# Norm factors of a differential attention spread over the partitions by TensorE transposes, with another planned order of the kernel's steps

## The chip, the cores and the metric

The kernel runs on one core of a Trainium2 chip. That core has five engines which run side by side, each through a list of instructions of its own in a fixed order: TensorE (PE, matrix products; PEld are its weight loads), VectorE (DVE), ScalarE (ACT), GpSimd (POOL), and SyncE (SP), which here issues the DMA transfers. An instruction that needs another engine's result waits for it, and everything behind it on the same engine waits too. The metric is the time of one execution on the device in microseconds (us); smaller is better.

## The reference, cut to what matters

One layer over 1024 positions of width 1024, in f32. One input projection feeds two groups of heads: group A (8 heads of 64) attends over its own chunk and 8 chunks to the left with a position bias, group B (4 heads of 128) subtracts two softmax maps, normalises each head's output by its root mean square, and both are gated, joined, projected and normalised.

```
s = q k^T * scale                  # two maps n = 0, 1 per head of group B
a = softmax(s0) - lam * softmax(s1)
o = a v                            # 128 values per head and position
o = o * rsqrt(mean(o^2) + eps) * subln_g * (1 - lam_init)
y_b = o * silu(g_b)
out = layer_norm(alpha * x + concat(y_a, y_b) @ w_out)
```

The rsqrt factor is one number per head and position.

## The kernel before, in words

Every f32 operand of a large product is split in a high part and a remainder (`xh` and `xl`, `wh` and `wl`, `pth` and `ptl`), and each product is made of two or three fast matmuls of such parts. ACT writes the high part (a cast), DVE or POOL subtracts it from the operand to give the remainder. A call on `nc.either` leaves it to the planner which of the two does it.

The program is first recorded and then ordered by a planner (`_Recorder`). Every operation gets a rank from its place in the recording (`SLOPE`), from the work that hangs on it and from its step's entry in `BIAS`; `_Recorder.schedule` then plays the program through with a cost for each operation and a delay, `HOP`, for a result that goes from one engine to another, and each engine takes the ready operation of the lowest rank. What comes out is the fixed order of each engine. `STEPS` names the steps in the order of recording: `qk_a0` to `qk_a3` project queries and keys of group A's four pairs of heads, `v_a`, `g_a` values and gates, `at_a` the attention, the same with `b` for group B, `wo` loads the output weights, `out0` makes group A's half of the output projection and `fin0` the other half with the last normalisation. Names of tiles carry their step's name: `at_b_ob` is tile `ob` of an `at_b` step, `qk_a_pj` the PSUM tile of a projection.

In an attention block the scores `sp` go to PSUM, DVE takes their maximum `nm`, ACT the exponent `p`; PE transposes `p` in 128x128 blocks into one PSUM bank `tp` (there is one buffer of it), ACT casts it to `pth`, DVE subtracts to `ptl`, and PE multiplies both with the values into `ya` (group A) or `ob` (group B). These two share one PSUM buffer (`yp`), so the next block's product starts only when the last reader of this one is through. While a block's chain runs over the other engines, PE does matmuls of other steps: projections, or `out_po` and `fin_po` of the output.

Group B's norm stands at the end of `attend_b`, once for each of four blocks of 256 positions and each of four heads, 16 times. ACT squares the output to `sq`, PE sums it over the partitions with a column of ones (so the sums stand with a position on each partition, `at_b_ob` 128x1), DVE scales them into `l0`, POOL raises them to the power -1/2. The output itself has its positions along the free dimension, so the factors must be spread as rows over all partitions: ACT multiplies the identity with each of two columns of `l0` (`dg`, two 128x128 diagonals), and PE multiplies a matrix of ones with both. DVE then applies the result to `yt`.

Of the kernel before, what the change touches and what calls it, by code (L numbers as in the profile page):

```python
# [12 lines left out]
F32 = mybir.dt.float32  # L13
# [5 lines left out]
P = 128  # L19
# [4 lines left out]
W = 512  # L24
# [4 lines left out]

HOP = dict(tensor=54, vector=36, scalar=36, gpsimd=80, sync=60)
ARRIVE = 1920.0
SLOPE = 165.1
CUTS = (0, 384, 512, 1024)
# [1 line left out]
LATE = 1600.0  # L37
SPARE = 420.0
BIAS = {
# [3 lines left out]
}  # L43

FIRST = "w0 x0 w2 w1 x1 w3 x2 x3 x4 x5 x6 x7".split()
WARM = 10
IN_TURN = {"m", "yp"}
BUFS = dict(small=5, y=4, stk=9, v=6, wr=4, wh=4, wl=4, p=4, ptl=2, pth=2, h=4, g=1, bt=1, tm=1, dg=1, s=2, yp=1, t=1, m=2)
STEPS = (
    "qk_a0 g_a0 init0 v_a0 g_a1 at_a0 qk_a1 at_a1 v_a1 qk_a2 g_a2 at_a2 qk_a3 g_a3 at_a3 qk_b0 g_b0 v_b0 "  # L50
    "at_b0 qk_b1 g_b1 at_b1 qk_b2 qk_b3 g_b2 v_b1 at_b2 g_b3 wo0 out0 wo1 at_b3 fin0"
).split()


# [89 lines left out]
def _cost(engine, fn, args, kw):  # L144

    out = args[0]
    n = out.width if isinstance(out, _View) else W
    psum = any(a.tile.psum for a in args if isinstance(a, _View))
    if engine == "tensor":
        if fn == "transpose":  # L150
            return 115, 190
        n = args[2].width
        if args[1].dtype == F32:
            return max(4 * n * 0.4167, 230), 205
        return max(11 + n * 0.4167, 112), 185
    if engine == "scalar":
        given = sum(isinstance(v, _View) for v in (*args[2:], kw.get("scale"), kw.get("bias"))) * 98
        n = max(n, args[1].width)
        return (65 if psum else 97) + 0.835 * n + given + (64 if "accum_out" in kw else 0), 100 + (50 if "accum_out" in kw else 0)
    if engine == "vector":  # L160
        if fn == "memset":
            return 25 + 0.1 * n, 85
        if fn in ("tensor_reduce", "bn_stats"):
            return 75 + 1.04 * args[1].width, 85
        if fn == "reciprocal":
            return 80 + 4 * n, 75
        if fn in ("tensor_scalar", "tensor_copy") and not psum:
            return 72 + 0.52 * n, 80
        return 72 + 1.04 * n, 85
    if engine == "gpsimd":  # L170
        if fn == "memset":
            return 40 + 0.9 * n, 50
        if fn == "tensor_scalar":
            return 250 + 0.84 * n + 83 * sum(isinstance(v, _View) for v in args[2:4]), 50
        if len(args) > 3 and args[3] == ALU.pow:
            return 500 + 85 * n, 40
        return 150 + 2.12 * n, 50
    return 50, 0
# [10 lines left out]
class _Recorder:  # L189
# [14 lines left out]
    def add(self, engine, fn, args, kw):  # L204
# [39 lines left out]
        for t in op.tiles:  # L244
            t.uses += 1
        (op.cost, op.lag), op.rank, op.start = _cost(engine, fn, args, kw), self.bias, None
        self.ops.append(op)

# [17 lines left out]
    def schedule(self):  # L266
# [19 lines left out]
        while len(order) < len(ops):  # L286
            again = False
            for e in self.ENGINES:
# [22 lines left out]
                if got.engine != e:  # L311
                    got.engine, (got.cost, got.lag) = e, _cost(e, got.fn, got.args, got.kw)
# [20 lines left out]
                for to in {x for s in got.succ for x in ops[s].either}:  # L333
                    heapq.heappush(events, (end if to == e else done + HOP[to], got.n, to))
                heapq.heappush(events, (done + (0 if e == "sync" else 60), got.n, "free"))
# [35 lines left out]
def hybrid_kernel(  # L371
# [18 lines left out]
    core, nc = tc.nc, _Recorder(tc)  # L390
# [3 lines left out]
    def pool(name, space="sbuf", bufs=None):  # L394
        n = bufs or BUFS[name]
        made = ctx.enter_context(tc.tile_pool(name="p_" + name, bufs=n, **spaces.get(space, {})))
        return _Pool(nc, made, n, space)
# [3 lines left out]
    y_pool, stk_pool, v_pool = pool("y"), pool("stk"), pool("v")  # L401
    wr_pool, wh_pool, wl_pool = pool("wr"), pool("wh"), pool("wl")
    p_pool, ptl_pool, pth_pool, h_pool, g_pool = pool("p"), pool("ptl"), pool("pth"), pool("h"), pool("g")
    bt_pool, tm_pool, dg_pool = pool("bt"), pool("tm"), pool("dg")
    sm_pool, st_pool = pool("small"), pool("stats", bufs=2)
    d_pool = pool("dram", "dram", 1)
    ps_s, ps_y, ps_m, ps_t = pool("s", "psum"), pool("yp", "psum"), pool("m", "psum"), pool("t", "psum")
# [1 line left out]
    ident = c_pool.tile([P, P], F32, "ident")  # L409
    make_identity(core, ident.get())  # L410
    ones = c_pool.tile([P, P], F32, "ones")
# [161 lines left out]
    def scores(stack, i, k0, w):  # L573

        q, k, kl = stack
        n = w if w <= W else W if w - W >= 256 else 384
        at = W - n if w > W else 0
        sp = ps_s.tile([P, 2 * W], F32, "sp", tag="s")
        block = slice(i * P, (i + 1) * P)
        for a, b in ((0, n), (n, w)):  # L580
            if a < b:
                keys, cols = slice(k0 + a, k0 + b), slice(at + a, at + b)
                nc.tensor.matmul(sp[:, cols], q[:, block], k[:, keys], start=True, stop=False)
                nc.tensor.matmul(sp[:, cols], q[:, block], kl[:, keys], start=False, stop=True)
        return sp[:, at : at + w]

    def exponent(sv, w, total):

        nm = sm_pool.tile([P, 1], F32, "nm", tag="nm")
        nc.vector.tensor_reduce(nm, sv, AX.X, ALU.max, negate=True)  # L590
        pt = p_pool.tile([P, S], F32, "p", tag="p")[:, :w]
        nc.scalar.activation(pt, sv, AF.Exp, bias=nm[:, 0:1], accum_out=total)
        return pt
# [66 lines left out]
    def attend_b(stacks, vt, yt):  # L660
        for g in range(4):
            ps = []
            l0, l1, cc = [sm_pool.tile([P, 2], F32, f"l{m}", tag=f"l{m}") for m in range(3)]
            for i in (2 * g, 2 * g + 1):
                w, u = (i + 1) * P, slice(i % 2, i % 2 + 1)
                es = []
                for m in range(2):
                    sv = scores(stacks[m], i, 0, w)
                    nc.vector.memset(sv[0:64, w - 64 : w], NEG)
                    es.append(exponent(sv, w, (l0, l1)[m][:, u]))  # L670

                p0, p1 = es
                nc.vector.reciprocal(l1[:, u], l1[:, u])
                nc.gpsimd.tensor_scalar(cc[:, u], l1[:, u], l0[:, u], nlam, ALU.mult, ALU.mult)
                nc.vector.scalar_tensor_tensor(p0, p1, cc[:, u], p0, ALU.mult, ALU.add)
                ps.append(p0)

            op = ps_y.tile([P, W], F32, "ob", tag="yp")
            o = op[:, :256]
            parts = []  # L680
            for k, us, hi, lo in transposed(ps, (0, 0), 2 * g + 2):
                parts += [(k, us, 0, hi), (k, us, 1, hi), (k, us, 0, lo)]
            for n, (k, us, part, pt) in enumerate(parts):
                nc.tensor.matmul(op[:, us], vt[k // 4][:, k % 4, part, :], pt, start=n == 0, stop=n == len(parts) - 1)

            cols = slice(g * 256, (g + 1) * 256)
            sq = tm_pool.tile([P, 256], F32, "sq", tag="tm")
            nc.scalar.square(sq, o)
            nc.vector.tensor_tensor(yt[:, cols], yt[:, cols], o, ALU.mult)
            nc.gpsimd.tensor_tensor(l0, l0, l0, ALU.mult)  # L690
            for u in range(2):
                nc.tensor.matmul(op[:, 256 + u : 257 + u], sq[:, u * P : (u + 1) * P], ones[:, 0:1], start=True, stop=True)

            nc.vector.scalar_tensor_tensor(l0, op[:, 256:258], 1.0 / (P * EPS), l0, ALU.mult, ALU.add)
            nc.gpsimd.tensor_tensor(l0, l0, mhalf, ALU.pow)
            dg = dg_pool.tile([P, 2, P], F32, "dg", tag="dg")
            for u in range(2):
                nc.scalar.mul(dg[:, u], ident, l0[:, u : u + 1])
            bc = op[:, 256:W]
            nc.tensor.matmul(bc.rearrange("p (u q) -> p u q", u=2), ones, dg, start=True, stop=True)  # L700
            nc.vector.scalar_tensor_tensor(yt[:, cols], yt[:, cols], gs[:, 0:1], bc, ALU.mult, ALU.mult)

    def gate(c0, yt):
# [73 lines left out]
    def at_b(p):  # L777
        attend_b(stacks["b", p], vb[p], yts["b", p])
# [173 lines left out]
```

## Time and profile before

| | us |
|---|---|
| median of 3 runs (679.42 to 681.44) | 679.81 |
| the profiled execution | 680.56 |
| its span, from the first to the last instruction | 678.8 |
| PE busy in it | 653.1 (96%) |
| PEld, DVE, ACT, POOL busy | 556.6, 410.0, 326.4, 328.9 |

The profiled execution's time is 1.8 us more than its span. A matmul's busy time includes a tail in which the next one already streams, so a busy PE may still have lost time between two starts. The granted clock of TensorE is 0.995 of full speed over the span; the slices of the page show it below 1.0 only at the very beginning and end.

### The profile page before, as it was taken

The page shows a single profiled execution, that of the slowest core. Times are in us where ns is not written, and L with a number is a line of the kernel's source. Part 1 is how long each engine was busy: PE and PEld are TensorE (multiplying, and loading weights), DVE is VectorE, ACT ScalarE, POOL GpSimd, SP SyncE. Part 2 cuts the span into 40 slices and gives each one's busy share as a digit, 9 for nine tenths or more (in the row PEclk, how much of TensorE's full clock was granted, in tenths as well). Part 3 has the DMA queues.
Part 4 walks back from the last instruction along what each step waited for, and adds up shares of the span by engine and source line. Part 5 has one row for each costly group of instructions (what it writes and reads, how often), then busy time and mean ns, then how long its engine had stood idle before and what let it go on. Part 6 is the DMA issues. An engine that isn't in the chain of part 4 may idle for free. (4 is left out here: it accounts for less than half of the span.)

```text
span 678.8 us, 10866 instructions
## 1 busy us (share of the span) xinstructions
PE 653.1 (96%) x3812; PEld 556.6 (82%) x3812; DVE 410.0 (60%) x839; ACT 326.4 (48%) x733; POOL 328.9 (48%) x367
## 2 busy tenths in 40 slices
PE   7899999999999999999999999999999999999993
PEld 7789878899888778787998788888798787878873
DVE  3521387777426764886248766842517957677875
ACT  5521466555335653665237546653416645454321
POOL 6620444434324443477225662677804736536673
PEclk8999999999999999999999999999999999999998
DMA  9433301400341125013320141125304643030121
GB/s 313 119 97 109 95 23 29 117 14 9 94 117 39 41 55 170 25 48 94 94 63 27 52 110 47 47 53 135 92 18 136 184 148 124 16 94 31 63 94 62
DMA packets 57855, 55.92 MB, mean 82 GB/s; under 512 B 5176, under 2 KB 44872, under 8 KB 57800
## 3 DMA queue, kind: packets, MB, share of 16 engines
q1 hardware_dynamic: 57800, 55.22, 27.1%
q8 instruction: 30, 0.49, 0.3%
q14 instruction: 25, 0.20, 0.1%
HBM read 36.32 MB, written 7.88 MB: 65 GB/s over the span
## 5 line engine op out<-in xcount | busy, mean ns | idle before, releaser
L367 POOL TENSOR_SCALAR at_a_p<-at_a_p,at_a_ls 128x640 f32<-128x640 f32 (+2 forms) x64 | 42.5, 666 | 49.2 <-DVE at_a_ls L367 42.0
L367 ACT ACTIVATE at_b_p<-at_b_sp,at_b_nm 128x128 f32<-128x128 f32 (+7 forms) x64 | 47.4, 743 | 26.3 <-DVE at_b_nm L367 20.4
L367 PE MATMUL fin_po<-wo_wo,fin_ys 128*128 128x512 f32 (+1 forms) x264 | 53.7, 356 | 4.0 <-DVE fin_z L367 2.7
L367 ACT ACTIVATE at_a_p<-at_a_sp,at_a_nm 128x640 f32<-128x640 f32 (+2 forms) x64 | 42.5, 664 | 24.8 <-DVE at_a_nm L367 15.2
L367 DVE TENSOR_TENSOR at_a_ptl<-at_a_tp,at_a_pth 128x512 fp32r<-128x512 f32 (+2 forms) x72 | 43.0, 597 | 16.1 <-ACT at_a_pth L367 15.2
L367 PEld LDWEIGHTS fin_po<-wo_wo,fin_ys 128*128 128x128 f32 x264 | 42.4, 189 | 10.9 <-DVE fin_z L367 3.2
L367 DVE TENSOR_REDUCE at_b_nm<-at_b_sp 128x1 f32<-128x128 f32 (+7 forms) x64 | 48.4, 757 | 2.1
L367 ACT CAST at_a_pth<-at_a_tp 128x512 fp32r<-128x512 f32 (+2 forms) x72 | 36.9, 512 | 22.1 <-PE at_a_tp L367 19.3
L367 PE MATMUL out_po<-wo_wo,out_ys 128*128 128x512 f32 x168 | 46.1, 404 | 0.0
L367 DVE TENSOR_REDUCE at_a_nm<-at_a_sp 128x1 f32<-128x640 f32 (+2 forms) x64 | 42.0, 656 | 1.7
L367 PE MATMUL at_a_ya<-at_a_pth,v_a_v 128*128 128x256 f32 x144 | 41.3, 287 | 1.4 <-DVE at_a_tm L367 0.9
L367 PE MATMUL at_a_tp<-k_ident,at_a_p 128*128 128x128 f32 x240 | 40.6, 279 | 1.0 <-DVE at_a_ptl L367 1.0
L367 POOL TENSOR_TENSOR g_a_ya<-g_a_ya,at_a_tm 64x256 f32<-64x256 f32 x32 | 23.9, 748 | 34.8 <-DVE at_a_tm L367 28.6
L367 PE MATMUL at_a_ya<-at_a_ptl,v_a_v 128*128 128x256 f32 x144 | 39.7, 305 | 0.4 <-DVE at_a_ptl L367 0.2
L367 PE MATMUL qk_b_pj<-k_xh,qk_b_wl 128*128 128x512 f32 x128 | 40.1, 403 | 0.0
L367 PE MATMUL qk_b_pj<-k_xl,qk_b_wh 128*128 128x512 f32 x128 | 39.0, 401 | 0.0
L367 PE MATMUL qk_b_pj<-k_xh,qk_b_wh 128*128 128x512 f32 x128 | 38.7, 401 | 0.0
L367 PE MATMUL v_b_pv<-v_b_wh,k_xh 128*128 128x256 f32 x128 | 36.3, 284 | 1.0 <-DVE g_b_yb L367 1.0
L367 PE MATMUL v_a_pv<-v_a_wh,k_xh 128*128 128x256 f32 x128 | 36.4, 284 | 0.0
L367 PE MATMUL v_a_pv<-v_a_wh,k_xl 128*128 128x256 f32 x128 | 36.3, 284 | 0.0
L367 PE MATMUL v_a_pv<-v_a_wl,k_xh 128*128 128x256 f32 x128 | 36.3, 283 | 0.0
L367 PE MATMUL v_b_pv<-v_b_wh,k_xl 128*128 128x256 f32 x128 | 36.2, 283 | 0.0
(170 smaller groups left out, 1912.0 us busy)
## 6 DMA issues: line engine op xcount, KB each, us to landing
xload_xr<-in_xt_dram SPq DMA_DIRECT2D x8, 512.0 KB, 7.4
qk_b_wr<-in_w_in_dram SPq DMA_DIRECT2D x16, 256.0 KB, 2.8
qk_b_r<-qk_b_r SPq DMA_DIRECT2D x64, 64.0 KB, 2.0
wo_wor<-in_w_out_dram SPq DMA_DIRECT2D x16, 256.0 KB, 2.7
out_z<-in_x_dram SPq DMA_DIRECT2D x14, 256.0 KB, 4.5
out_dram<-out_z SPq DMA_DIRECT2D x14, 256.0 KB, 2.0
qk_a_wr<-in_w_in_dram SPq DMA_DIRECT2D x12, 256.0 KB, 2.7
g_a_wr<-in_w_in_dram SPq DMA_DIRECT2D x8, 256.0 KB, 3.2
```

The costliest lines, as they stand in the source:

```text
L367: fn(*[real(a) for a in o.args], **{k: real(a) for k, a in o.kw.items()})
```

## The change

The spread of the factors loses ACT's two multiplications, the tile `dg` and the product with ones. Instead, PE transposes twice: its operand is a column of `l0` read with a step of zero along the free dimension, so each of 128 columns is the same one, and the transpose (against the identity, as for `p`) writes the factors as rows on all partitions, at the same place in PSUM. The rest of the chain is unchanged.

The planner's delay to TensorE rises from 54 to 304, so it plans every operand from another engine to reach PE 250 ns later; its cost of a transpose goes from 115 to 110. Four entries of `BIAS` change, and `STEPS` is reordered: `at_a0` is recorded ahead of `g_a1`, `v_a1` ahead of `at_a1`, `v_b1` ahead of `qk_b3` and `g_b2`.

```
-HOP = dict(tensor=54, vector=36, scalar=36, gpsimd=80, sync=60)
+HOP = dict(tensor=54 + 250, vector=36, scalar=36, gpsimd=80, sync=60)
...
-    "qk_a0 g_a0 init0 v_a0 g_a1 at_a0 qk_a1 at_a1 v_a1 qk_a2 g_a2 at_a2 qk_a3 g_a3 at_a3 qk_b0 g_b0 v_b0 "
+    "qk_a0 g_a0 init0 v_a0 at_a0 g_a1 qk_a1 v_a1 at_a1 qk_a2 g_a2 at_a2 qk_a3 g_a3 at_a3 qk_b0 g_b0 v_b0 "
...
         if fn == "transpose":
-            return 115, 190
+            return 110, 190
...
             nc.gpsimd.tensor_tensor(l0, l0, mhalf, ALU.pow)
-            dg = dg_pool.tile([P, 2, P], F32, "dg", tag="dg")
+
+            bc = op[:, 256:W]
             for u in range(2):
-                nc.scalar.mul(dg[:, u], ident, l0[:, u : u + 1])
-            bc = op[:, 256:W]
-            nc.tensor.matmul(bc.rearrange("p (u q) -> p u q", u=2), ones, dg, start=True, stop=True)
+                wide = l0[:, u : u + 1].custom(lambda r: r.to_broadcast([P, P]))
+                nc.tensor.transpose(bc[:, u * P : (u + 1) * P], wide, ident)
             nc.vector.scalar_tensor_tensor(yt[:, cols], yt[:, cols], gs[:, 0:1], bc, ALU.mult, ALU.mult)
```

PE issues 16 products with ones less and 32 transposes more, ACT 32 multiplications less; every other operation is there as before, in another order from some point on. PE's order is the same for its first 347 instructions and its last 211. Where the planner chose between DVE and POOL, seven operations in all moved to POOL, among them one of sixteen `k_xl` at the start and two of 28 operations `out_z<-out_z,fin_gb` of the last normalisation.

The first place is the start of the program on POOL, where the remainders of `x` are made (`xr` is a loaded piece of `x`; numbers are buffers, `k_xl_216` and `xload_xr_153` of before are `k_xl_211` and `xload_xr_150` now).

```order
L367 TENSOR_TENSOR k_xl_178<-xload_xr_150,k_xh_172 128x2x256
L367 TENSOR_TENSOR k_xl_216<-xload_xr_153,k_xh_207 128x2x256
L367 TENSOR_TENSOR k_xl_286<-xload_xr_156,k_xh_275 128x2x256
L367 TENSOR_TENSOR k_xl_216<-xload_xr_153,k_xh_207 128x2x256
L367 TENSOR_TENSOR k_xl_307<-xload_xr_159,k_xh_296 128x2x256
L367 TENSOR_TENSOR k_xl_286<-xload_xr_164,k_xh_275 128x2x256
```

The same place on POOL now:

```order
L367 TENSOR_TENSOR k_xl_175<-xload_xr_147,k_xh_169 128x2x256
L367 TENSOR_TENSOR k_xl_211<-xload_xr_150,k_xh_202 128x2x256 x2
L367 TENSOR_TENSOR k_xl_290<-xload_xr_153,k_xh_278 128x2x256
L367 TENSOR_TENSOR k_xl_308<-xload_xr_156,k_xh_292 128x2x256
L367 TENSOR_TENSOR k_xl_290<-xload_xr_161,k_xh_278 128x2x256
```

Both halves of the piece `xload_xr_150` (153 before) now follow each other, ahead of the next piece. On ACT the casts of this piece moved in the same way: the first stands ahead of the two `qk_a_q` instead of behind them, the second between `qk_a_q` and `qk_a_k` instead of behind two casts of the next piece. On DVE one `k_xl` instead of two stands ahead of the two `qk_a_kl`.

The second place is the end of group A's attention on PE, in the last block of step `at_a3`, from the last transpose of a bank to the first of the next; `g_b_pj` is a projection that fills the time.

```order
L367 MATMUL at_a_tp_3667<-k_ident_123,at_a_p_3575 128x128
L367 MATMUL at_a_ya_3658<-at_a_ptl_3656,v_a_v_1686 128x256
L367 MATMUL at_a_ya_3658<-at_a_pth_3651,v_a_v_2064 128x256
L367 MATMUL at_a_ya_3658<-at_a_ptl_3656,v_a_v_2064 128x256
L367 MATMUL g_b_pj_3679<-k_xh_172,g_b_wh_3304 128x512 x3
L367 MATMUL at_a_ya_3658<-at_a_pth_3677,v_a_v_2064 128x256
L367 MATMUL g_b_pj_3679<-k_xh_172,g_b_wh_3304 128x512
L367 MATMUL g_b_pj_3679<-k_xl_178,g_b_wh_3304 128x512 x4
L367 MATMUL g_b_pj_3679<-k_xh_172,g_b_wl_3328 128x512
L367 MATMUL at_a_tp_3704<-k_ident_123,at_a_p_3552 128x128
```

The same place on PE now:

```order
L367 MATMUL at_a_tp_3696<-k_ident_120,at_a_p_3574 128x128
L367 MATMUL at_a_ya_3693<-at_a_ptl_3687,v_a_v_1524 128x256
L367 MATMUL at_a_ya_3693<-at_a_pth_3681,v_a_v_1632 128x256
L367 MATMUL at_a_ya_3693<-at_a_ptl_3687,v_a_v_1632 128x256
L367 MATMUL g_b_pj_3642<-k_xh_202,g_b_wh_3370 128x512 x4
L367 MATMUL at_a_ya_3693<-at_a_pth_3704,v_a_v_1632 128x256
L367 MATMUL g_b_pj_3642<-k_xl_211,g_b_wh_3370 128x512 x2
L367 MATMUL at_a_tp_3720<-k_ident_120,at_a_p_3549 128x128
```

Four filling matmuls instead of three stand between the transposes and the first product that reads their cast, and two instead of six between that product and the next transposes into the one bank.

The third place is the last norm of group B on PE, from the sums of squares to the spread (`fin_po` is the output projection of `fin0`).

```order
L367 MATMUL at_b_ob_6921<-k_ones_132,at_b_sq_7000 128x1 x2
L367 MATMUL fin_po_7006<-wo_wo_6407,fin_ys_6629 128x512
L367 MATMUL fin_po_7006<-wo_wo_6419,fin_ys_6629 128x512 x3
L367 MATMUL fin_po_7006<-wo_wo_6453,fin_ys_6629 128x512 x3
L367 MATMUL fin_po_7034<-wo_wo_6364,fin_ys_6727 128x512 x3
L367 MATMUL fin_po_7034<-wo_wo_6407,fin_ys_6727 128x512
L367 MATMUL at_b_ob_6921<-at_b_dg_7037,k_ones_132 128x256
```

The same place on PE now:

```order
L367 MATMUL at_b_ob_6891<-k_ones_129,at_b_sq_6981 128x1 x2
L367 MATMUL fin_po_6966<-wo_wo_6419,fin_ys_6586 128x512
L367 MATMUL fin_po_7001<-wo_wo_6340,fin_ys_6683 128x512 x3
L367 MATMUL fin_po_7001<-wo_wo_6380,fin_ys_6683 128x512 x3
L367 MATMUL at_b_ob_6891<-k_ident_120,at_b_l_1348_6702 128x128 x2
```

Seven filling matmuls instead of eleven stand between the sums and the spread. On POOL, three remainders `fin_ys` of 128x128 now stand between the three `out_z` and this norm's power; before, the power came right behind the `out_z`.

## Rows read from the trace of the kernel before

**Rows 1.** The page, busy time of each engine, share, instructions.

```profile
PE 653.1 (96%) x3812; PEld 556.6 (82%) x3812; DVE 410.0 (60%) x839; ACT 326.4 (48%) x733; POOL 328.9 (48%) x367
```

**Rows 2.** Busy time by window: PE, PEld, DVE, ACT, POOL; clock; DMA; GB/s.

```profile
0.00:20.00 20.00, 15.25 (x86) 14.20 (x86) 7.84 (x9) 12.56 (x23) 13.29 (x16) 0.91 0.95 318
...
660.00:680.00 20.00, 7.83 (x61) 7.22 (x60) 10.55 (x21) 2.14 (x3) 5.61 (x5) 0.88 0.21 79
```

**Rows 3.** Waits of PE's weight loads: us in total, times, longest.

```profile
PEld at_a_ya L367 <- ACT at_a_pth L367: 7.0, 23, 0.7
PEld at_a_sp L367 <- ACT at_a_p L367: 5.0, 16, 0.5
PEld at_a_tp L367 <- DVE at_a_ptl L367: 5.0, 12, 1.2
PEld at_b_sp L367 <- ACT at_b_p L367: 4.9, 16, 0.7
PEld at_b_ob L367 <- ACT at_b_dg L367: 3.5, 6, 1.4
...
PEld at_a_ya L367 <- DVE at_a_ptl L367: 3.1, 12, 0.4
PEld at_b_ob L367 <- ACT at_b_pth L367: 2.1, 2, 1.5
```

**Rows 4.** Timeline of PE at the start: start us, us, instruction, [idle before].

```profile
20.33 0.50 PE L367 MATMUL qk_a_pj<-k_xl,xload_wh 128*128 128x256 f32 x2 [1.25 <-POOL k_xl L367]
...
21.88 0.71 PE L367 MATMUL qk_a_pj<-k_xh,xload_wh 128*128 128x256 f32 x4 [0.57 <-DVE qk_a_kl L367]
```

**Rows 5.** Timeline at the start: ACT, DVE and POOL.

```profile
11.52 1.14 ACT L367 CAST k_xh<-xload_xr 128x512 fp32r<-128x512 f32 x2 [0.43 <-DMA xload_xr<-in_xt_dram]
...
15.19 0.62 ACT L367 CAST k_xh<-xload_xr 128x512 fp32r<-128x512 f32 x1
...
17.79 3.04 DVE L367 TENSOR_TENSOR k_xl<-xload_xr,k_xh 128x512 fp32r<-128x512 f32 x2 [1.71 <-ACT k_xh L367]
...
15.89 9.48 POOL L367 TENSOR_TENSOR k_xl<-xload_xr,k_xh 128x512 fp32r<-128x512 f32 x6 [1.09 <-ACT k_xh L367]
```

**Rows 6.** Tiles dg and tp of group B: count, ns min/median/max, first and last start.

```profile
L367 ACT ACTIVATE at_b_dg<-k_ident,at_b_l x32: 386/402/409, 365.9 to 626.6; 128x128 f32<-128x128 f32 x32
...
L367 PE MATMUL at_b_ob<-at_b_dg,k_ones x32: 377/379/483, 366.9 to 627.4; 128*128 128x256 f32 x32
...
L367 PE MATMUL at_b_tp<-k_ident,at_b_p x144: 270/272/330, 354.1 to 619.7; 128*128 128x128 f32 x144
```

**Rows 7.** Timeline of PE: one product with ones, four transposes.

```profile
565.55 0.59 PE L367 MATMUL at_b_ob<-at_b_dg,k_ones 128*128 128x256 f32 x2
...
312.95 0.60 PE L367 MATMUL at_a_tp<-k_ident,at_a_p 128*128 128x128 f32 x4
```

**Rows 8.** Timeline around the last norm of group B: PE, POOL, ACT.

```profile
624.09 2.78 PE L367 MATMUL fin_po<-wo_wo,fin_ys 128*128 128x512 f32 x11
627.07 0.70 PE L367 MATMUL at_b_ob<-at_b_dg,k_ones 128*128 128x256 f32 x2 [0.20 <-ACT at_b_dg L367]
...
621.35 4.23 POOL L367 TENSOR_TENSOR out_z<-out_z,fin_gb 128x512 f32<-128x512 f32 x3 [0.75 <-ACT out_z L367]
625.54 0.75 POOL L367 TENSOR_TENSOR at_b_l<-at_b_l,k_mhalf 128x2 f32<-128x2 f32 x1
626.26 0.87 POOL L367 TENSOR_TENSOR fin_ys<-g_b_yb,fin_ys 128x128 fp32r<-128x128 f32 x2
...
626.32 0.69 ACT L367 ACTIVATE at_b_dg<-k_ident,at_b_l 128x128 f32<-128x128 f32 x2 [3.31 <-POOL at_b_l L367]
```

**Rows 9.** Timeline of the tail: DVE, then PE.

```profile
657.13 2.88 DVE L367 TENSOR_TENSOR out_z<-out_z,fin_gb 128x512 f32<-128x512 f32 x2 [0.28 <-ACT out_z L367]
...
662.98 3.14 PE L367 MATMUL fin_po<-wo_wo,fin_ys 128*128 128x256 f32 x24 [1.43 <-DVE fin_z L367]
```

More of the change, by code (lines that the diff above doesn't have):

```diff
@@ L47 @@
 IN_TURN = {"m", "yp"}
-BUFS = dict(small=5, y=4, stk=9, v=6, wr=4, wh=4, wl=4, p=4, ptl=2, pth=2, h=4, g=1, bt=1, tm=1, dg=1, s=2, yp=1, t=1, m=2)
+BUFS = dict(small=5, y=4, stk=9, v=6, wr=4, wh=4, wl=4, p=4, ptl=2, pth=2, h=4, g=1, bt=1, tm=1, s=2, yp=1, t=1, m=2)
 STEPS = (
-    "qk_a0 g_a0 init0 v_a0 g_a1 at_a0 qk_a1 at_a1 v_a1 qk_a2 g_a2 at_a2 qk_a3 g_a3 at_a3 qk_b0 g_b0 v_b0 "
-    "at_b0 qk_b1 g_b1 at_b1 qk_b2 qk_b3 g_b2 v_b1 at_b2 g_b3 wo0 out0 wo1 at_b3 fin0"
+    "qk_a0 g_a0 init0 v_a0 at_a0 g_a1 qk_a1 v_a1 at_a1 qk_a2 g_a2 at_a2 qk_a3 g_a3 at_a3 qk_b0 g_b0 v_b0 "
+    "at_b0 qk_b1 g_b1 at_b1 qk_b2 v_b1 qk_b3 g_b2 at_b2 g_b3 wo0 out0 wo1 at_b3 fin0"
 ).split()
@@ L403, in hybrid_kernel @@
     p_pool, ptl_pool, pth_pool, h_pool, g_pool = pool("p"), pool("ptl"), pool("pth"), pool("h"), pool("g")
-    bt_pool, tm_pool, dg_pool = pool("bt"), pool("tm"), pool("dg")
+    bt_pool, tm_pool = pool("bt"), pool("tm")
     sm_pool, st_pool = pool("small"), pool("stats", bufs=2)
```

6 rows, old and new, of the table BIAS are left out of this document.

## The prediction

> **What bounds the kernel now.** I read the page first: PE is busy 96% of the span, the other engines at most 60% [rows 1]. PE is the bound, but how it loses time matters, since the change takes away less than 1% of its work. The windows come next: PE is short of full in the first 20 us (15.25 us busy) and in the last (7.83) [rows 2]; between them it is nearly full. That is only part of the truth. A matmul's recorded time holds a tail under which the next one streams: four transposes take 0.60 us and one takes 0.272 [rows 6, 7], so they start (0.60 - 0.272) / 3 = 0.109 us apart, and the tail is 0.16. A wait shorter than the tail does not show as idle PE. So I read the waits of the weight loads, which stand ahead of the matmuls [rows 3]. Each counts for what it has over 0.16 us. The seven rows shown hold 30.6 us in 87 waits, so 30.6 - 87 x 0.16 = 16.7 us of PE in the attention steps: many waits of some tenths of a microsecond, not one large one. The reader should see three stocks to draw on: PE's own work, these small waits, and the waits at the start and in the tail.
>
> **What the change is worth, part by part.** All terms are changes to the profiled execution's 680.56 us, 0.75 above the median of the runs.
>
> Work of PE. One product with ones is two records of 379 ns, and the two take 0.59 us, so they start 0.59 - 0.379 = 0.21 us apart [rows 6, 7]; 32 records are 32 x 0.21 = 6.7 us. The 32 transposes at 0.109 are 3.5 us. PE is the bound wherever they stand, so the term is **-3.2**. What no row shows is a transpose whose stationary operand is read with step zero. If it cost as much as a record of the product with ones (the nearest dearer row), the term would be 0; I see no reason for a gain beyond -3.2. I take the transposes' own row, because the shape, type and identity operand are theirs, and step zero reads no more columns.
>
> The Trainium skill (TensorE: Matmul & The Clock Gate, Part 4: PE-mode transpose) gives a transpose about 275 ns in one kernel's context, with the access latency as most of it. The trace has 272 for one, which agrees, but also the four in a row, which do not queue up for 275 each. Taken as occupancy, that figure of the Trainium skill would make 32 x 0.275 = 8.8 us, and the term +2.1 instead of -3.2.
>
> ACT. 32 multiplications of 402 ns go, 12.9 us [rows 6]. ACT is at 48% and this is worth nothing by itself. What it shortens is the chain: the pair took 0.69 us between POOL's power and PE [rows 8]. It also stood in ACT's queue waiting for that power (3.31 us in the row), and casts behind it waited too. In its place PE now waits for POOL directly, and all of PE's queue stands behind that wait. This is the term that can turn against the change. Counted over the whole printed order, with 0.23 us for a 512-wide matmul (11 in 2.78 us [rows 8]), PE had a median of 3.8 us of work between the sums of squares and the spread at the 16 places, and has 2.2 now; the five shortest are 1.6 us. Take the last one: the power ended at 625.54 + 0.75 = 626.29, 2.2 us after the sums (624.09), and PE now comes after 7 x 0.23 = 1.6. That is a wait of 0.6 us even if POOL is no later, and 1.9 if the three `fin_ys` (0.87 / 2 = 0.44 each) now ahead of the power count in full. Before, PE waited 0.2 there. Over all 16 places the weight loads' waits for `dg` were worth 3.5 - 6 x 0.16 = 2.5 us [rows 3]. I charge **+1.0** on balance: 0.4 to 1.7 at this place, little at those where POOL is free. The bounds are -2.5 (all these waits vanish) and, as a rival below, many times +1.
>
> Start. PE waits 1.25 us for a `k_xl` of POOL at 20.33 and 0.57 for DVE's `qk_a_kl` at 21.88 [rows 4]. POOL does six `k_xl` from 15.89 on, 1.58 us each [rows 5], and PE's is the third. Now it is the second, and does not wait for a cast behind `qk_a_k`. Its cast takes ACT's slot at 15.19 (0.62 us, so done at 15.8), and POOL, which was free 1.09 us before 15.89, does the first half from 14.8 and this one from about 16.4 to 18.0, against PE's need at 20.33 - 1.25 = 19.1: the first wait is gone. DVE has one `k_xl` of 3.04 / 2 = 1.5 us ahead of `qk_a_kl` instead of two, so that comes 1.5 us earlier, for a PE that is 1.25 us earlier: the second wait shrinks by 0.25 more. Together 1.5, plus 0.2 for a smaller wait on the cast: **-1.7**. The cover is ACT's idle time: the first cast of that piece now stands ahead of two `qk_a_q`. The piece before it was cast at 11.52 as it landed; a piece is 512 KB, which at 318 GB/s [rows 2] takes 1.6 us, so it lands near 13.2, in time. Were it to land only when ACT cast it, at 15.19, `qk_a_q` would be 1.4 us late and the term near 0. POOL does one `k_xl` more, ahead of its weight remainders; they are needed when PE's first projections are done, several us later.
>
> Small waits of the attention steps. Planning operands 250 ns later puts more filling matmuls between a producer and PE's use. Over the printed order of group A, PE's work from the last transpose of a bank to the first product with its cast goes from a median of 1.00 us to 1.29, and 38 of 72 places have under 1.3 us instead of 58. This touches the waits of `at_a_ya` and `at_b_ob` for `pth` and `ptl`: 12.2 us in 37 waits, worth 12.2 - 37 x 0.16 = 6.3. I take two thirds, **-4.0**, since the mean wait (0.33) is about the distance added (0.29) and the longest, 1.5 us, stay. The other rows, `at_a_tp`, `at_a_sp` and `at_b_sp` (14.9 us in 44 waits, worth 7.9), hang on one bank of `tp` and two of `sp`; the distance from bank to bank does not grow (median 1.86 to 1.87 for `tp` in group A), and at the second place shown it falls from 2.5 us of work to 1.8. I count 0 for them, between -3 and +3. The moved steps swap which projections fill which attention and cost nothing by themselves: the same matmuls, and the weight loads' waits name no transfer.
>
> Tail. PE's last 211 instructions keep their order, so the long waits there stay unless DVE changes. Two of the `out_z` multiplications left DVE; one of them stood in the pair of 2.88 us at 657.13, ahead of the evacuation of PE's next bank. That is 1.4 us less on DVE, of which POOL's longer queue takes some back through the power that DVE waits for; the wait of 1.43 at 662.98 [rows 9] shrinks by some 0.9, and an earlier one may grow by 0.3: **-0.6**, between -1.4 and +0.4.
>
> **The sum.** -3.2 + 1.0 - 1.7 - 4.0 - 0.6 = -8.5; 680.56 - 8.5 = 672.1 against the profiled execution, 679.81 - 8.5 = 671.3 against the median, which I forecast.
>
> **The rivals.** (1) *The added distance buys nothing*: a fixed stock of filling work is only spread otherwise, and each wait avoided at a product returns at the one bank of `tp`. For it: the second place shown. Against it: the start, where PE is short, is unaffected, and the counts of short places fall without a rise elsewhere. Then the -4.0 is lost: 675.3. (2) *The spread doesn't get cheaper*, because step zero makes a transpose cost what a record of the product cost: +3.2, 674.5; if a transpose holds PE for its full 0.272 us, 32 x (0.272 - 0.109) = +5.2, 676.5. Against both: the 144 transposes of `p` in group B [rows 6], which stream like any matmul. The second form is what the Trainium skill (TensorE: Matmul & The Clock Gate, Part 4: PE-mode transpose) would give if its duration is read as occupancy. (3) *Slower: PE waits for POOL's power.* Place: the transposes at the end of the 16 blocks. POOL works in order and an operation of it takes 0.44 to 1.4 us [rows 8]; one of 1.4 us ahead of the power at each place is 16 x 1.4 = 22 us, less the 1.0 already charged: 671.3 + 21 = 692. It decides from (8.5 + 1.0) / 16 = 0.6 us for each place on. For it: this is where the distance shrank by 1.6 us in the median and only 0.69 us of chain went. Against it: the planner counts POOL's queue too, and before, with the same rules, only 6 of 16 places waited [rows 3]. A mild form, 0.3 us each, ends at 671.3 + 3.8 = 675.1. (4) *No change that can be told*: the order's gain at the start is eaten by the late load (+1.7), rival 1 holds (+4.0), and the power costs another 2 us: 679.
>
> **How the numbers follow.** A difference under 0.3%, 2.0 us, can't be told from none. Chances: forecast 0.55, with a range of its own from 667 to 675 from the bounds of the small waits and the power; rival 1 0.16; rival 2 0.10 in both forms; a mild or strong rival 3 0.11, of which 0.06 end slower than 681.8; rival 4 0.08. Faster by over 0.3% (below 677.8): forecast, rivals 1 and 2 and the mild rival 3, 0.86; within 0.3%: 0.08; slower: 0.06. The range of 8 in 10 goes from 664.5, where the small waits give 8, the start 2 and the tail 1.4, and the power's waits give a part of their 2.5 (-3.2 - 8 - 2 - 1.4 - 0.7 = -15.3, 664.5), to 678.0, which takes in rivals 1, 2 and the mild 3.
>
> **What would show it.** Right: transposes of 270 to 275 ns in `at_b_ob`, four or two of them 0.11 us apart; no wait of PE for `k_xl` at 20 us, and all of PE about 1.7 us earlier at 25 us; weight loads' waits for `at_a_pth` well under 7.0 us; PE's busy time near 650. Wrong: PE waits for POOL's `at_b_l` that sum to several us; waits for `at_a_ptl` before `at_a_tp` above 5.0 us; a transpose of `l0` longer than one of `p`; a wait at 16 us for `qk_a_k` that grows.

## The result, and the profile after

The changed kernel took 669.89 us in the median, the kernel before 680.44 us beside it: a ratio of 0.9839 [0.9813, 0.9865], 11.0 us less. Two more comparisons gave 0.9808 [0.9774, 0.9841] and 0.9839 [0.9805, 0.9874]. The forecast was 671.3 us, 8.5 less than before. The trace that came with this result is of an execution that ran at a granted clock of 0.655 throughout (887.78 us), so the rows of after are of run r1_after_again, the same kernel, whose profiled execution took 667.92 us, 12.6 less than that of before (680.56).

The page's busy times, which answer to [rows 1], and the windows, which answer to [rows 2] (the last one is the last 20 us of the span):

```profile
PE 642.7 (96%) x3812; PEld 551.5 (83%) x3812; DVE 401.3 (60%) x832; ACT 316.1 (47%) x701; POOL 339.7 (51%) x374
```

```profile
0.00:20.00 20.00, 15.00 (x99) 13.63 (x100) 8.72 (x11) 14.43 (x27) 15.23 (x18) 1.00 0.97 321
20.00:40.00 20.00, 20.00 (x98) 16.92 (x98) 6.32 (x12) 6.57 (x12) 9.58 (x7) 1.00 0.35 100
...
646.10:666.10 20.00, 9.63 (x75) 8.95 (x73) 11.83 (x21) 2.13 (x3) 7.98 (x7) 0.92 0.21 79
```

PE did 99 matmuls in the first 20 us where it did 86, at a clock of 1.00 where it was 0.91. Its busy time fell by 10.4 us, three times the 3.2 of work removed: a busy time holds the tails under which short waits hide, so fewer waits show there too, and the execution of before ran at half clock for a while (last section).

The waits of PE's weight loads, which answer to [rows 3] (us in total, times, longest us):

```profile
PEld at_a_tp L367 <- issue: 5.3, 15, 0.8
PEld at_a_tp L367 <- DVE at_a_ptl L367: 4.7, 16, 0.7
PEld at_b_sp L367 <- ACT at_b_p L367: 4.6, 14, 0.9
PEld at_a_ya L367 <- ACT at_a_pth L367: 4.2, 9, 1.3
PEld at_a_sp L367 <- ACT at_a_p L367: 3.4, 13, 0.4
...
PEld at_b_tp L367 <- DVE at_b_ptl L367: 2.4, 7, 0.4
PEld at_b_ob L367 <- POOL at_b_l L367: 1.8, 2, 1.3
...
PEld at_b_ob L367 <- DVE at_b_ptl L367: 1.4, 2, 1.2
```

The row of `at_a_ya` for `at_a_ptl` (3.1 us, 12 times) and that of `at_b_ob` for `at_b_pth` (2.1) are gone; 23 waits for `at_a_pth` are 9. One row has grown: 15 waits of `at_a_tp` for "issue", for which the profile names no one. Before they were two:

```profile
PEld at_a_tp L367 <- issue: 0.7, 2, 0.4
```

The waits of PE itself in the same execution:

```profile
PE fin_po L367 <- DVE fin_z L367: 2.2, 2, 1.3
...
PE at_b_ob L367 <- POOL at_b_l L367: 0.9, 1, 0.9
PE fin_po L367 <- DVE out_z L367: 0.7, 1, 0.7
```

PE waits once for POOL's power in 16 places. The two rows of the tail were 2.7 and 1.3.

The start, which answers to [rows 4] and [rows 5] (start us, us, instruction, idle before): PE, then ACT, DVE and POOL.

```profile
14.82 0.71 PE L367 MATMUL qk_a_pj<-k_xh,xload_wh 128*128 128x256 f32 x4 [1.20 <-ACT qk_a_k L367]
...
19.15 0.71 PE L367 MATMUL qk_a_pj<-k_xh,xload_wh 128*128 128x256 f32 x4 [1.22 <-DVE qk_a_kl L367]
...
22.09 1.09 PE L367 MATMUL qk_a_pj<-k_xh,xload_wh 128*128 128x512 f32 x4
```

```profile
13.79 0.62 ACT L367 CAST k_xh<-xload_xr 128x512 fp32r<-128x512 f32 x1
...
16.39 1.01 DVE L367 TENSOR_TENSOR k_xl<-xload_xr,k_xh 128x512 fp32r<-128x512 f32 x1 [1.72 <-ACT k_xh L367]
17.43 0.42 DVE L367 TENSOR_TENSOR qk_a_kl<-qk_a_pj,qk_a_k 64x256 fp32r<-64x256 f32 x1
18.57 0.43 DVE L367 TENSOR_TENSOR qk_a_kl<-qk_a_pj,qk_a_k 64x256 fp32r<-64x256 f32 x1 [0.72 <-POOL k_xl L367]
...
12.63 8.84 POOL L367 TENSOR_TENSOR k_xl<-xload_xr,k_xh 128x512 fp32r<-128x512 f32 x6
...
15.55 1.29 POOL L367 TENSOR_TENSOR k_xl<-xload_xr,k_xh 128x512 fp32r<-128x512 f32 x1
```

The wait for `k_xl` at 20 us is gone. The remainder that ended it was the third of POOL's six from 15.89 on [rows 5]; in the new row, which begins one remainder earlier in the order, it is again the third (the line at 15.55, an excerpt of the row of six) and is done at 16.84. The waits for `qk_a_k` (0.8 us before, in PE's list) and for `qk_a_kl` (0.57) have grown to 1.2 each; the second `qk_a_kl` had itself stood 0.72 us on DVE, by the profile for a `k_xl` of POOL. PE reaches its first 512-wide group at 22.09. Before it did so here:

```profile
24.82 1.09 PE L367 MATMUL qk_a_pj<-k_xh,xload_wh 128*128 128x512 f32 x4
```

The last norm of group B, which answers to [rows 8]: PE, then POOL.

```profile
614.24 1.88 PE L367 MATMUL fin_po<-wo_wo,fin_ys 128*128 128x512 f32 x7
615.96 0.38 PE L367 MATMUL at_b_ob<-k_ident,at_b_l 128*128 128x128 f32 x2
...
613.56 1.30 POOL L367 TENSOR_TENSOR fin_ys<-g_b_yb,fin_ys 128x128 fp32r<-128x128 f32 x3
614.82 0.72 POOL L367 TENSOR_TENSOR at_b_l<-at_b_l,k_mhalf 128x2 f32<-128x2 f32 x1
```

The power ends at 615.54, PE comes at 615.96 and waits for nothing. The three `fin_ys` that the prediction placed ahead of the power are there, but POOL had begun them before the sums of squares were done.

### The profile page after: what moved, and what is told of

It reads as the page before. It is cut to its first block, busy times and chain, and to the rows that moved or that the text cites. A ratio compares the mean times of both kernels' runs of the same rounds, so it can differ in the third digit from the quotient of the medians.

```text
span 886.0 us, 10802 instructions
## 1 busy us (share of the span) xinstructions
PE 874.5 (99%) x3812; PEld 684.3 (77%) x3812; DVE 399.0 (45%) x832; ACT 317.5 (36%) x701; POOL 333.4 (38%) x374
## 4 chain that ended last, share of the span: by engine, by line
PE 98%; DVE 1%; DMA 1%; SPq 0%; DVEq 0%; issue 0%; ACT 0%
PE qk_b_pj L367 14%; PE qk_a_pj L367 14%; PE fin_po L367 8%; PE v_b_pv L367 7%; PE g_b_pj L367 7%; PE v_a_pv L367 7%; PE g_a_pj L367 7%; PE out_po L367 6%; PE at_b_ob L367 6%; PE at_b_sp L367 5%; PE at_a_ya L367 5%; PE at_a_sp L367 5%; PE at_a_tp L367 4%; PE at_b_tp L367 3%; DMA xload_wr<-in_w_in_dram 1%; DVE fin_z L367 0%
## 5 line engine op out<-in xcount | busy, mean ns | idle before, releaser
L367 PE MATMUL fin_po<-wo_wo,fin_ys 128*128 128x512 f32 (+1 forms) x264 | 74.3, 452 | 1.0 <-DVE fin_z L367 1.0
L367 PEld LDWEIGHTS fin_po<-wo_wo,fin_ys 128*128 128x128 f32 x264 | 50.5, 224 | 18.3 <-issue 4.5
L367 PE MATMUL out_po<-wo_wo,out_ys 128*128 128x512 f32 x168 | 61.1, 514 | 0.0
L367 PE MATMUL at_a_tp<-k_ident,at_a_p 128*128 128x128 f32 x240 | 56.3, 340 | 0.0
L367 PE MATMUL qk_b_pj<-k_xh,qk_b_wl 128*128 128x512 f32 x128 | 52.9, 509 | 0.0
L367 PE MATMUL qk_b_pj<-k_xl,qk_b_wh 128*128 128x512 f32 x128 | 51.8, 516 | 0.0
L367 PEld LDWEIGHTS at_a_tp<-k_ident,at_a_p 128*128 128x128 f32 x240 | 34.9, 159 | 16.4 <-issue 6.6
L367 DVE TENSOR_TENSOR at_a_sp<-at_a_sp,at_a_bt 128x256 f32<-128x256 f32 (+1 forms) x64 | 26.5, 414 | 45.5 <-PE at_a_sp L367 44.9
L367 PEld LDWEIGHTS out_po<-wo_wo,out_ys 128*128 128x128 f32 x168 | 34.7, 216 | 13.7 <-issue 3.5
L367 ACT CAST at_b_pth<-at_b_tp 128x512 fp32r<-128x512 f32 (+1 forms) x40 | 21.7, 543 | 63.5 <-PE at_b_tp L367 59.7
L367 PE MATMUL v_b_pv<-v_b_wl,k_xh 128*128 128x256 f32 x128 | 44.0, 344 | 0.0
```

The costliest lines, as they stand in the source:

```text
L367: fn(*[real(a) for a in o.args], **{k: real(a) for k, a in o.kw.items()})
```

## The experiments

Each kernel was timed in five rounds beside the kernel before. "Less" is the ratio's distance from 1 times the median of before in the same comparison (682.9 us for the first four runs, 681.7 and 680.8 for the next two fours). The last two columns are of the profiled execution alone. PE's first 116 matmuls are the same in all these kernels; "wide at" is where the next one, its first 512-wide group, starts, and "rest" is the time from there to the end of the span.

| run | what it is | median us | ratio | less, us | wide at | rest |
|---|---|---|---|---|---|---|
| before | as it was | | | | 24.82 | 654.0 |
| e1_after | changed kernel | 669.16 | 0.9808 [0.9774, 0.9841] | 13.1 | 25.75 | 644.2 |
| e2_spread_only | before + transposes | 677.94 | 0.9932 [0.9903, 0.996] | 4.6 | 23.67 | 649.0 |
| e3_lag_only | before + distance | 677.07 | 0.9921 [0.9892, 0.9949] | 5.4 | 21.48 | 650.4 |
| e4_after_no_lag | changed, no distance | 678.33 | 0.9927 [0.9898, 0.9956] | 5.0 | 22.45 | 649.5 |
| r1_after_again | changed kernel | 669.79 | 0.9839 [0.9805, 0.9874] | 11.0 | 22.09 | 644.0 |
| r2_after_old_spread | changed, old spread | 671.76 | 0.9872 [0.9837, 0.9906] | 8.7 | 22.35 | 647.8 |
| r3_spread_and_lag | before + both | 667.77 | 0.9817 [0.9783, 0.9851] | 12.5 | 21.76 | 644.0 |
| r4_spread_twice | changed, spread doubled | 671.65 | 0.9868 [0.9836, 0.99] | 9.0 | 21.83 | 647.6 |
| r5_lag_early | distance in the start only | 674.12 | 0.9906 [0.9887, 0.9926] | 6.4 | 24.25 | 649.6 |
| r6_lag_late | distance after it only | 670.50 | 0.9841 [0.9819, 0.9863] | 10.8 | 27.00 | 644.1 |
| r7_lag500 | changed, twice the distance | 666.64 | 0.9798 [0.9776, 0.982] | 13.8 | 21.84 | 642.7 |
| r8_slow_power | changed, power 0.6 us later | 671.48 | 0.9868 [0.9845, 0.989] | 9.0 | 25.09 | 646.3 |

"Wide at" differs by 3.7 us between two executions of the changed kernel (25.75 and 22.09; the last section shows what went with it), and their times with it (671.75 and 667.92 us). "Rest" does not: the granted clock is 1.00 from 24 us to the tail, and the two executions of the changed kernel differ by 0.2 us. So it prices an edit better than the medians do, but leaves out what the edit does at the start.

The theory is the prediction's: less PE work, and small waits of the attention removed by the added distance, with a charge for POOL's power. The rivals are those of the prediction.

**The parts, one by one.** e1_after is the changed kernel as it is.

> The changed kernel again, for a trace at the full clock. My theory (all parts of the change share in the gain: 3 us of PE work, 1.7 us at the start, 4 us of small waits) expects 669 to 671 us against 680; PE busy near 650; transposes of the column 0.11 us apart; PE's wait for k_xl at 20 us gone; the weight loads' waits of at_a_ya for at_a_pth near 3 us instead of 7.0, those of at_a_tp for at_a_ptl unchanged near 5. The rival (the planner's delay buys nothing, a wait avoided at a product comes back at the single bank of tp) expects at_a_tp's waits above 7 us.

e2_spread_only puts the transposes into the kernel before:

```
-            for u in range(2):
-                nc.scalar.mul(dg[:, u], ident, l0[:, u : u + 1])
             bc = op[:, 256:W]
-            nc.tensor.matmul(bc.rearrange("p (u q) -> p u q", u=2), ones, dg, start=True, stop=True)
+            for u in range(2):
+                wide = l0[:, u : u + 1].custom(lambda r: r.to_broadcast([P, P]))
+                nc.tensor.transpose(bc[:, u * P : (u + 1) * P], wide, ident)
```

> The kernel before with the transposes in place of the product with ones, and nothing else (old delay, steps, biases). My theory expects the saved PE work alone, 3.2 us less, and up to 1 us lost to waits for POOL's power: a ratio of 0.995 to 0.997 (676.7 to 678). The rival that a step of zero makes the transpose dear expects no gain, 0.999 to 1.001. A second rival, that the shorter chain is worth more than the work, expects 0.992 or less.

e3_lag_only has the distance alone, and e4_after_no_lag takes it out of the changed kernel (the reverse edit):

```
-HOP = dict(tensor=54, vector=36, scalar=36, gpsimd=80, sync=60)
+HOP = dict(tensor=54 + 250, vector=36, scalar=36, gpsimd=80, sync=60)
```

> The kernel before with the planner's delay to TensorE raised from 54 to 304, and nothing else. My theory expects the start (1.7 us) and the small waits (4 us): a ratio of 0.990 to 0.993 (673 to 675.5). The rival that the added distance buys nothing expects the start alone, 0.997 to 0.998 (678.5).

> The changed kernel with the planner's delay put back to 54, the rest of the change kept. My theory expects it 5 to 6 us slower than the changed kernel (675 to 676, a ratio of 0.992 to 0.994 to before). The rival that the delay buys only the start expects 671 to 672 (0.987).

By the ratios the spread alone is worth 4.6 us, the distance alone 5.4, and taking the distance out of the changed kernel costs 13.1 - 5.0 = 8.1. Past the start it is 654.0 - 649.0 = 5.0, 654.0 - 650.4 = 3.6 and 649.5 - 644.1 = 5.4 (644.1 stands for the 644.0 and 644.2 of the changed kernel). The 8.1 holds some of the scatter: the profiled execution of e4_after_no_lag took 673.73 us at a granted clock of 0.995, its other eight 675.21 to 680.09 at 0.987 to 0.991, where the six of e1_after had 0.991 to 0.997. Whether the missing distance lowers the clock there is not shown.

The spread alone gave more than its theory (a ratio of 0.995 to 0.997). Of the 5.0 us, 3.2 are PE's work, and the power takes some back; the other waits of the attention steps fell from 18.3 to 16.3 us, counted as in the prediction over all their rows, and one of 0.9 for `g_b_yb` went. So the rival of the shorter chain had a part in it.

Waits of the weight loads in e2_spread_only, e3_lag_only and e4_after_no_lag, in this order:

```profile
PEld at_a_ya L367 <- ACT at_a_pth L367: 6.7, 22, 0.7
...
PEld at_b_ob L367 <- POOL at_b_l L367: 4.9, 9, 1.3
```

```profile
PEld at_a_ya L367 <- ACT at_a_pth L367: 4.2, 8, 1.0
...
PEld at_b_ob L367 <- ACT at_b_dg L367: 2.8, 5, 0.8
```

```profile
PEld at_b_ob L367 <- POOL at_b_l L367: 7.4, 9, 1.5
...
PEld at_a_ya L367 <- ACT at_a_pth L367: 6.4, 22, 0.7
...
PEld at_a_ya L367 <- DVE at_a_ptl L367: 4.2, 12, 0.9
```

The distance thins the waits for `at_a_pth`; the spread leaves them. Without the distance the spread makes PE wait for POOL's power: 4.9 - 9 x 0.16 = 3.5 us in e2_spread_only, 7.4 - 9 x 0.16 = 6.0 in e4_after_no_lag. With it, 1.8 - 2 x 0.16 = 1.5 are left. So the distance does more in the changed kernel than by itself, and the mild rival 3 was real and hidden by it. In time the first two rivals fall: the distance buys 5.4 us alone, and the spread 4.6.

**Steps and biases, and the spread inside the change.** r2_after_old_spread is the changed kernel with the product with ones back, the reverse of the diff of e2_spread_only. r3_spread_and_lag is the kernel before with the two edits above; it has neither the moved steps nor the new biases, nor the new cost of a transpose.

> The changed kernel once more, beside the parts of this call. Both theories expect 667.5 to 671.8 us as before, ratio 0.978 to 0.985. The one long wait at the start of the first profile (2.7 us for xload_wh) should not come back if it was the chance of a late load; if the change causes it, it stands there again. Weight loads' waits at_a_ya for at_a_pth should be 9 or so, near 4.1 us, and PE's waits for POOL's at_b_l near 1.0 us.

> The changed kernel with the product with ones put back (32 multiplications of ACT and 16 products), order and lag as changed. Theory A, the prediction's terms: the spread is worth 3.2 us of PE's work and takes back 1.0 through POOL's power, so 2.2 us more than the changed kernel, some 671.3. Theory B, the waits of the spread were a gain and not a loss: 4.5 to 5.5 us more, 673.7 to 674.7, with weight loads waiting for dg some 6 times. Theory C, the lag and the steps do nearly all: 669 to 670.

> The kernel before with the transposes and the lag of 304, but the steps and biases of before. Theory A, the parts add up and steps and biases do nothing: 4.6 + 5.4 = 10 us less than before, 1.5 to 3 us above the changed kernel at most because of the start, so 670 to 672. Theory B, the steps and biases are worth 3 us together with the lag: 672 to 673. If POOL's power were what the steps had to mend, PE's waits for at_b_l would be several us here against 1.0 in the changed kernel.

r3_spread_and_lag is not slower than the changed kernel (12.5 us against 11.0 beside it), so the moved steps and biases bring nothing that can be told; past the start the two are level (both 644.0). Nor do they bring anything without the distance (5.0 against 4.6). The old spread costs 11.0 - 8.7 = 2.3 us, beside 2.2 in the prediction, but the two intervals overlap over half their width. Past the start it costs 647.8 - 644.1 = 3.7, more than the 3.2 of work: there the power takes nothing back. The long wait at the start that stood in e1_after did not come back in r1_after_again; see the last section.

**The price of one transpose.** r4_spread_twice writes each spreading transpose twice into the same place:

```
                 nc.tensor.transpose(bc[:, u * P : (u + 1) * P], wide, ident)
+                nc.tensor.transpose(bc[:, u * P : (u + 1) * P], wide, ident)
```

> The changed kernel with each of the 32 spreading transposes written twice into the same place, so 32 more of them with nothing else added: it prices one. Theory A, a step-zero transpose streams like the others, 0.109 us: 3.5 us more, 672.6. Rival, it costs a record of the product, 0.21 us: 6.7 us more, 676. Rival, it holds PE for its 0.272 us: 8.7 us more, 678. In the trace the four in a row should start 0.11 us apart under the first theory and 0.27 under the last.

The tile's row in r1_after_again, then in r4_spread_twice the page's busy times and one of its sixteen groups of four:

```profile
L367 PE MATMUL at_b_ob<-k_ident,at_b_l x32: 270/272/323, 361.3 to 616.1; 128*128 128x128 f32 x32
```

```profile
PE 645.9 (96%) x3844; PEld 555.2 (83%) x3844; DVE 401.7 (60%) x837; ACT 315.5 (47%) x701; POOL 333.2 (50%) x369
```

```profile
361.30 0.60 PE L367 MATMUL at_b_ob<-k_ident,at_b_l 128*128 128x128 f32 x4
```

A transpose of a column with step zero lasts 272 ns, as one of `p` does [rows 6], and four take 0.60 us, so they start (0.60 - 0.272) / 3 = 0.109 us apart. The 32 added ones cost PE 645.9 - 642.7 = 3.2 us of busy time and 669.5 - 666.1 = 3.4 of span (3.6 past the start, where PE waits for the power at two places more); the medians differ by 1.9. The first theory had 3.5. The figure of the Trainium skill (TensorE: Matmul & The Clock Gate, Part 4: PE-mode transpose), some 275 ns, agrees with the duration of one here, 272, and is not what PE is held for: read as occupancy, it would have made 32 x 0.272 = 8.7 us in place of the 3.4.

**Where the distance works.** It is given only to operands that the planner has ready before 25 us of its own time (r5_lag_early), or only after that (r6_lag_late, with `<=`):

```
-heapq.heappush(events, (end if to == e else done + HOP[to], got.n, to))
+heapq.heappush(events, (end if to == e else done + HOP[to] - (250 if to == "tensor" and done > 25000 else 0), got.n, to))
```

> The changed kernel with the added distance of 250 ns only for operands that the planner has ready in its first 25 us; after that 54 as before. Theory A, the prediction's split: the start is worth 1.7 us and the attention steps' small waits 4.0, so this keeps the smaller part: 4 us above the changed kernel, some 673.5 to 674.5 us, ratio 0.988 to 0.990, with weight loads waiting 20 times or more for at_a_pth. Rival, the distance works at the start alone: 669 to 671 and the attention waits don't matter. Rival, it works in the attention alone: 676 to 678, as without the added distance.

> The reverse: the added distance only after the planner's first 25 us. Theory A: the 1.7 us of the start is lost and the 4.0 of the attention stays, 671 to 672 us, ratio 0.984 to 0.987; PE waits 1.3 us for k_xl at 20 us again, and the weight loads wait about 9 times for at_a_pth. Rival, the start is all: 676 to 678. Rival, the attention is all: 669 to 670.

Late alone keeps 10.8 of the 11.0 to 13.1 us, early alone 6.4, little more than the 5.0 without any distance. Past the start the two kernels lie 649.6 - 644.1 = 5.5 us apart. At the start, the wait for `k_xl` is back in r6_lag_late, and not in r5_lag_early:

```profile
22.51 0.50 PE L367 MATMUL qk_a_pj<-k_xl,xload_wh 128*128 128x256 f32 x2 [1.27 <-POOL k_xl L367]
```

Weight loads of r5_lag_early, then of r6_lag_late:

```profile
PEld at_b_ob L367 <- POOL at_b_l L367: 7.6, 10, 1.5
PEld at_a_ya L367 <- ACT at_a_pth L367: 6.5, 22, 0.7
...
PEld at_a_ya L367 <- DVE at_a_ptl L367: 4.2, 12, 0.8
```

```profile
PEld at_a_tp L367 <- issue: 5.3, 15, 0.8
...
PEld at_a_ya L367 <- ACT at_a_pth L367: 4.1, 9, 1.2
...
PEld at_b_ob L367 <- POOL at_b_l L367: 1.9, 2, 1.4
```

By 0.16 us each, the waits for the power fall from 6.0 to 1.6 us and those of `at_a_ya` from 3.0 + 2.3 to 2.7; the "issue" row takes back 5.3 - 15 x 0.16 = 2.9, and others of the attention steps rise too (`at_b_sp` for `at_b_p` from 0.9 to 2.4). Over all rows past the start the attention steps' waits rise, from 15.4 to 17.0 us. So of the 5.5 us the power gives 4.4 and the tail 1.1 (4.8 to 3.8), the attention's waits take back 1.6, and the remaining 1.6 lie in gaps too short for the list.

**More distance.** r7_lag500 has `tensor=54 + 500`.

> The changed kernel with 500 ns of added distance in place of 250. If the remaining waits of the weight loads in the attention steps (some 20 us in 65 waits, worth about 10) hang on the distance too, another third of them goes: 666 to 667 us. If they hang on the one bank for the transposes and the two for the scores, nothing: 669 to 670. If the filling work is used up, waits come back elsewhere, above all for POOL's power ahead of the spread and in the last 40 us: 671 to 674.

666.64 us is the lowest median of all the kernels, 14 us below before. Its interval is clear of none of the three of the changed kernel, so that it beats that one too is likely and not shown by the times; past the start it is 1.3 to 1.5 us shorter in the traces. Its weight loads:

```profile
PEld at_a_tp L367 <- DVE at_a_ptl L367: 5.6, 17, 0.6
PEld at_a_sp L367 <- ACT at_a_p L367: 4.3, 13, 0.5
PEld at_b_sp L367 <- ACT at_b_p L367: 3.9, 13, 0.8
PEld at_a_tp L367 <- issue: 3.7, 10, 0.6
...
PEld at_b_ob L367 <- POOL at_b_l L367: 2.8, 3, 1.3
PEld at_a_ya L367 <- ACT at_a_pth L367: 1.6, 3, 1.0
```

The waits for `at_a_pth` go on falling (9 to 3). Those of `at_a_tp` for `at_a_ptl` and of `at_a_sp`, which the prediction hung on one bank and on two, rise a little. What is left in group A's attention is mostly theirs.

**How near the slower rival is.** r8_slow_power puts two multiplications by one ahead of each power:

```
+            for _ in range(2):
+                nc.gpsimd.tensor_scalar(l0, l0, 1.0, 1.0, ALU.mult, ALU.mult)
             nc.gpsimd.tensor_tensor(l0, l0, mhalf, ALU.pow)
```

> The changed kernel with two multiplications by one on POOL ahead of each of the 16 powers, some 0.3 us each: 0.6 to 0.7 us more between the sums of squares and the spread at every place, which is what the prediction's slower rival asked for as the point from which it decides. Theory A, the power is covered by filling work at nearly all places: at most 1 us more than the changed kernel, PE waiting for at_b_l at one or two places more. Rival, PE stands behind the power at each place: 16 x 0.65 = 10 us more, 680.

POOL's busy time rose from 339.7 to 348.7 us, 0.28 for each of the 32, so 0.56 at a place. PE's wait and that of its weight loads, from two lists of this run:

```profile
PE at_b_ob L367 <- POOL at_b_l L367: 2.7, 4, 1.1
```

```profile
PEld at_b_ob L367 <- POOL at_b_l L367: 4.8, 5, 1.5
```

Three more places wait, and the waits for the power are worth 4.8 - 5 x 0.16 = 4.0 us against 1.5. In the table the kernel is 2.0 us above r1_after_again, whose ratio is of another comparison; past the start it is 646.3 - 644.1 = 2.2. The 16 x 0.56 = 9 us do not show: at 11 places filling work covers the later power. The first theory's "at most 1 us" was too low.

## Why the prediction was right

Forecast, range and sign held; the gain was 2.5 us larger than forecast (11.0 against 8.5). That it came so near is in part luck: terms that were off in both directions stand beside gains that nobody had foreseen. Term by term, against the profiled execution of r1_after_again (12.6 us less; the fastest of its six, 1.9 under their median), each wait of a weight load counted above 0.16 us:

- *Work of PE, -3.2.* Right, by row and by r4_spread_twice: 0.109 us for each, 3.2 to 3.4 for 32. Rival 2 had no place.
- *POOL's power, +1.0.* Wrong in sign. The waits for the factors went from 2.5 us (for `dg`) to 1.5 (for `at_b_l`): -1.0. The charge fits the spread without the distance: 3.5 - 2.5 = +1.0 in e2_spread_only. At the last place the prediction let the power end 2.2 us after the sums, as before, with PE back after 1.6, and so found 0.6 to 1.9 us of wait. The rows after have the power's end at 615.54 - 614.24 = 1.3 and PE's return at 615.96 - 614.24 = 1.7. PE's distance was counted well, POOL's lateness was not; and that the distance after the start is what took these waits away is shown by r5_lag_early against r6_lag_late.
- *Start, -1.7.* Right for one wait of two, and too large. The `k_xl` wait went (-1.25), but `qk_a_kl`, forecast to shrink, grew by 0.65, and `qk_a_k` by 0.4, which the text had put down as a sign of being wrong. By these three rows 0.2 us are left. PE's first wide group comes 2.7 earlier, because this execution also had a shorter wait for a load and no stretch at half clock (below). By r6_lag_late the distance at the start is worth 0.2 to 2.3. The nearest like pair of traces gives 1.0: e4_after_no_lag without the distance and e3_lag_only with it both waited under 0.2 us for that load, at a clock of 1.00, and reach the wide group at 22.45 and 21.48.
- *Small waits of the attention, -4.0.* Right for the rows it named, wrong for the sum. The waits for `pth` and `ptl` in question fell from 6.3 us to 4.2 - 9 x 0.16 = 2.8, -3.5. `at_a_tp`, `at_a_sp` and `at_b_sp`, held at 0, fell from 7.9 to 5.8, but "issue" at `at_a_tp` rose from 0.7 - 2 x 0.16 = 0.4 to 2.9, and rows that the prediction does not name rose as well (`at_a_tp` for `at_a_p` of POOL from nothing to 0.8, `at_b_ob` for `at_b_ptl` from 0.4 to 1.1). All rows of the attention steps together fell from 18.3 us (101 waits) to 16.8 (89): -1.5. So rival 1 was much of it: most of what goes at the products comes back, above all at the transposes into the one bank.
- *Tail, -0.6.* The two rows of PE's list fell from 4.0 to 2.9, -1.1, inside its bounds.
- *Not foreseen.* A wait of PE for `g_b_yb` ahead of `v_b_pv`, 1.0 us once, is gone. It is gone in e2_spread_only too, which has the steps of before, so the moved `v_b1` is not needed for it.

Past the start, all waits of the weight loads together fell from 44.2 us in 112 to 37.2 in 95, by the 0.16 us from 26.3 to 22.0, so by 4.3: 1.5 in the attention steps, 1.0 for the factors, 0.8 in the tail and 0.9 for `g_b_yb`. With the 2.7 of the start and the 3.2 of work that makes 10.2 of the 12.6. The other 2.4 lie in gaps between matmuls that are too short for the list, and what they waited for is not shown.

## What to carry over

A scheduler that plans operands a little too early leaves waits that no busy share shows; most of them stand in the list of the weight loads' waits, and telling the planner a later time is a one-number change that is worth trying at two or three values (250 and 500 ns gave 5.4 and 649.5 - 642.7 = 6.8 us past the start here). Add up all rows of such a list before crediting a gain to some of them: waits that leave one row come back in another. Judge a new dependency, such as PE on POOL's power, together with the order in which it will run: the same spread cost 6.0 us of waits without the distance and 1.5 with it. Take the price of an operation from how far apart four in a row start, not from the duration of one. Where the start of a program scatters, compare from a point that all kernels reach by the same work.

## What was not expected of the hardware

PE's granted clock in the first 25 us differs between executions of one kernel, and a long idle time of PE mostly goes ahead of a fall. Windows (their columns as in [rows 2]) and PE's wait in the execution of e1_after:

```profile
8.00:10.00 2.00, 0.00 (x0) 0.00 (x0) 0.00 (x0) 1.02 (x2) 0.46 (x1) 0.77 0.83 260
10.00:12.00 2.00, 1.73 (x8) 1.74 (x9) 1.10 (x1) 1.22 (x3) 1.11 (x2) 0.50 0.95 292
12.00:14.00 2.00, 2.00 (x11) 2.00 (x11) 1.35 (x1) 1.57 (x4) 2.00 (x2) 0.50 1.00 259
```

```profile
10.27 0.80 PE L367 MATMUL qk_a_pj<-k_xh,xload_wh 128*128 128x256 f32 x2 [2.68 <-ACT xload_wh L367]
```

PE had waited 2.68 us for a loaded weight's cast, and ran at 1.2 GHz (0.50) from before 10 to 14 us and longer; in r1_after_again, the same kernel, this wait was 0.40 us and the clock 1.00 in the first 40 us. In the kernel before it was 1.05, and the clock 0.50 from 10 to 12 us. The wait was long again in r5_lag_early, r6_lag_late and r8_slow_power (2.21, 2.14 and 2.28 us), each time with a clock of 0.50 from 10 to 12 us; in the other traces it was 0.61 at most, and there the clock did not fall behind it. At half clock a group of four 256-wide matmuls takes 1.05 us instead of 0.64. The profiled executions of the two kernels thus differ by more than the change: 3.7 us lie between the arrivals of e1_after (25.75) and r1_after_again (22.09) at the same wide group. Waits of 1.2 us at 14.8 and 19.2 us in r1_after_again brought no fall; and the 1.30 us for `k_xl` at 18 us brought one in e2_spread_only (0.50 from 20 to 22 us) and none in e4_after_no_lag, so the length of one wait does not settle it. What makes the load come late in some executions stays open, as does what the 15 "issue" waits of `at_a_tp` stand for.
